# Sums of squares over the partitions: one product in single precision, or two products of the split type

## The chip, the cores and the metric

One core of a Trainium2 chip runs the whole program. The metric is the device time of one execution in microseconds (us); several executions are timed and their median is quoted. One further execution is recorded by the hardware profiler, with its instructions, its waits and its transfers. All durations below come from that one record.

## The reference, cut to what matters

The program is one layer of an encoder on 2,176 tokens (2,048 of a prompt, 128 of running streams) of width 1,024. Every row norm has the same form:

```python
def rmsnorm(x, g):
    xf = x.astype(jnp.float32)
    y = xf * lax.rsqrt(jnp.mean(xf * xf, axis=-1, keepdims=True) + RMS_EPS)
    return (y * g.astype(jnp.float32)).astype(x.dtype)
```

A token is normed before the input projection; the attention output and the pooling mixer's output are normed separately before they go into one output projection; the sum with the residual is normed before a squared-ReLU network of width 4,096; its result is normed before a gate; and the final result is normed once more. Everything is float32.

## The kernel before, in words

Tokens lie along the free axis and channels over the 128 partitions, so a sum of squares over channels is a sum over partitions and over tiles. All weights and activations of the large products are split into a high part (rounded to the type fp32r) and a low part (the rest), and `mm3` (L166 to L171) makes each product as three fp32r products: high by high, low by high, high by low. `split` (L179 to L181) makes the two parts: ScalarE (ACT) copies into the high part (L180), and VectorE (DVE) or GpSimd (POOL) subtracts (L181).

The program has two stages. **Stage A** goes over six blocks of tokens (one of 256, five of 384): `load_norm` (L251) loads and norms, then the input projection, attention, the pooling mixer, and `out_proj` (L275). A string (L27) lays out by hand in which order the pieces of the blocks are written. In its last letters the mixer of block 5 (`B5`) and the attention's rest of block 5 (`A5`) come ahead of the last piece of the output projection of block 4 (`O4`). **Stage B** works on six parts (four of 368 tokens, two of 352), in three pairs: an up projection that combines blocks of weights and activations (`up`), a down projection, a tail with the gate, and a finish that norms and writes out. The tail of one pair lies beside the up projection of the next.

The class `SumSq` does every norm's sum. `add` (L188): ACT squares a tile into a temporary `sqt` (L198), POOL or DVE adds it to the accumulator `sqa` (L199). When all tiles are in, `rstd` (L226) or `rstd_dve` (L201) adds over the partitions: TensorE (PE) multiplies by a matrix of ones (L229, L204) into a bank of PSUM called `ms`, of which there is one. Then comes the reciprocal root: in `rstd_ps`, ACT takes a logarithm (L236) and an exponential (L237) and DVE corrects in three steps (L238 to L240); in `rstd_dve`, DVE does it all in eleven steps (L208 to L215).

There are 35 such sums: five in the prologues of blocks 1 to 5, three in each of six output projections (`out_ra`, `out_rb` and the sum of the projected rows, two of the last kind run in stage B), six of the tail's and six of the finish, of which three go by `rstd_dve` and three by `rstd`. Block 0's prologue makes its products in a line of its own (L659).

Temporaries rotate through a fixed number of buffers by tag, in the order in which the program is written: `sqt` has 2 (the up projection's `v` takes from the same two), `sqa` 5, the rows of x (tag `xr`) 4, and `rt` 2 (the root's temporaries, shared with operands of `up`). A tile can be written only when the earlier tile of its buffer has been read for the last time. The order of each engine's instructions is not the program's: a scheduler lays it out from its own model of durations, within the dependencies and the rotation. Once laid out, an engine runs its list strictly in order. All loads stand in one list, that of SyncE (SP).

## Time and profile before

| | us |
|---|---|
| median of 3 runs (2475.68 to 2479.82) | 2478.29 |
| the profiled execution | 2475.05 |
| its span, first to last instruction | 2473.3 |
| PE busy in the span | 2341.9 (95%) |
| DVE busy | 1718.6 (69%) |
| POOL busy | 1154.7 (47%) |
| ACT busy | 1027.8 (42%) |

The span is what the profile can explain; 1.75 us lie outside it. PE is busy nearly everywhere, so a stretch is read by where PE is not: stage A (to about 780 us), the step from stage A to stage B (690 to 780), the two changeovers between pairs (about 1325 to 1400 and 1905 to 1965), and the end (from 2452).

### The profile page before, as it was taken

What the parts mean: (1) busy time and instruction counts of PE and PEld (TensorE: products, weight loads), DVE (VectorE), ACT (ScalarE), POOL (GpSimd) and SP (SyncE); (2) the same over time, 40 slices, a digit from 0 to 9 for tenths busy, and PEclk for the clock granted to TensorE, in tenths of its full rate; (3) what the DMA queues carried; (4) which work ended last, traced back from release to release, by engine and by line L of the source; (5) the groups of instructions that cost most, each with busy time, mean ns of one, the idle gap of its engine ahead of it and who ended that gap; (6) DMA issues with size and microseconds to landing.
All of it is one profiled execution on the core that took longest, in us unless ns stands there. A gap on an engine that the chain in (4) does not pass through costs nothing. (4 is left out here: it accounts for less than half of the span.)

```text
span 2473.3 us, 39045 instructions
## 1 busy us (share of the span) xinstructions
PE 2341.9 (95%) x13748; PEld 2258.1 (91%) x13748; DVE 1718.6 (69%) x3050; ACT 1027.8 (42%) x2139; POOL 1154.7 (47%) x964
## 2 busy tenths in 40 slices
PE   7879898999979999999998999999999899999996
PEld 7868797788879999999998999999999899999996
DVE  6866678767858777766677777776577866666565
ACT  5545555445633333332454333333365223333364
POOL 5734355434565444433475344443277333333275
PEclk9989999999999999999999999999999999999998
DMA  7554586688482334432455234342355522222233
GB/s 181 166 190 154 160 271 204 219 284 298 151 300 94 112 122 125 126 94 69 163 188 166 93 124 123 121 133 73 128 184 148 159 69 76 74 73 69 86 99 107
DMA packets 235443, 356.99 MB, mean 144 GB/s; under 512 B 43120, under 2 KB 119664, under 8 KB 235248
## 3 DMA queue, kind: packets, MB, share of 16 engines
q1 hardware_dynamic: 234704, 353.78, 45.5%
q8 instruction: 109, 1.79, 0.3%
q14 instruction: 86, 0.70, 0.1%
q10 hardware_dynamic: 544, 0.72, 0.1%
HBM read 284.86 MB, written 69.55 MB: 143 GB/s over the span
## 5 line engine op out<-in xcount | busy, mean ns | idle before, releaser
L181 POOL TENSOR_TENSOR wlo<-wraw,whi 128x512 fp32r<-128x512 f32 x277 | 380.9, 1381 | 308.6 <-ACT whi L180 234.0
L169 PE MATMUL ps_dn<-hh,whi 128*128 128x368 f32 (+1 forms) x1536 | 505.6, 329 | 8.4 <-DVE acc L881 7.6
L170 PE MATMUL ps_dn<-hh,wlo 128*128 128x368 f32 (+1 forms) x1536 | 503.6, 328 | 0.0
L171 PE MATMUL ps_dn<-hl,whi 128*128 128x368 f32 (+1 forms) x1536 | 501.3, 327 | 0.0
L180 ACT CAST whi<-wraw 128x512 fp32r<-128x512 f32 x436 | 267.7, 618 | 308.7 <-PE ps_dn L171 89.3
L881 DVE TENSOR_TENSOR acc<-ps_dn,acc 128x368 f32<-128x368 f32 (+1 forms) x384 | 201.5, 530 | 268.1 <-PE ps_dn L171 266.6
L181 POOL TENSOR_TENSOR wlo<-A,whi 128x512 fp32r<-128x512 f32 x96 | 126.9, 1322 | 383.8 <-ACT whi L180 278.6
L169 PEld LDWEIGHTS ps_dn<-hh,whi 128*128 128x128 f32 x1536 | 288.3, 188 | 17.4 <-DVE acc L881 16.3
L170 PEld LDWEIGHTS ps_dn<-hh,wlo 128*128 128x128 f32 x1536 | 288.4, 188 | 0.6 <-DVE wlo L181 0.3
L171 PEld LDWEIGHTS ps_dn<-hl,whi 128*128 128x128 f32 x1536 | 288.4, 188 | 0.3
L180 ACT CAST whi<-A 128x512 fp32r<-128x512 f32 x192 | 118.7, 620 | 271.3 <-PE ps_dn L171 185.8
L169 PE MATMUL ps_in<-xnh,whi 128*128 128x384 f32 (+1 forms) x480 | 164.8, 343 | 19.7 <-DVE z L698 10.3
L199 POOL TENSOR_TENSOR sqa<-sqa,sqt 128x384 f32<-128x384 f32 (+3 forms) x119 | 132.4, 1114 | 91.5 <-ACT sqt L198 83.0
L180 ACT CAST whi<-S 128x512 fp32r<-128x512 f32 x144 | 89.2, 619 | 183.7 <-PE ps_dn L171 133.2
L170 PE MATMUL ps_in<-xnh,wlo 128*128 128x384 f32 (+1 forms) x480 | 162.0, 337 | 0.3 <-DVE wlo L181 0.3
L171 PE MATMUL ps_in<-xnl,whi 128*128 128x384 f32 (+1 forms) x480 | 161.1, 337 | 0.3 <-DVE xnl L246 0.3
L181 DVE TENSOR_TENSOR wlo<-wraw,whi 128x512 fp32r<-128x512 f32 x159 | 139.1, 875 | 17.4 <-ACT whi L180 15.4
L817 POOL TENSOR_TENSOR S<-A,S 128x512 f32<-128x512 f32 x48 | 62.8, 1308 | 139.8 <-DVE wlo L181 139.8
L170 PE MATMUL ps_gt<-x2h,wlo 128*128 128x368 f32 (+1 forms) x384 | 126.6, 330 | 0.0
L169 PE MATMUL ps_gt<-x2h,whi 128*128 128x368 f32 (+1 forms) x384 | 126.1, 328 | 0.0
L171 PE MATMUL ps_gt<-x2l,whi 128*128 128x368 f32 (+1 forms) x384 | 125.5, 327 | 0.0
L181 DVE TENSOR_TENSOR wlo<-S,whi 128x512 fp32r<-128x512 f32 x144 | 105.7, 734 | 21.0 <-ACT whi L180 17.1
(254 smaller groups left out, 6341.6 us busy)
## 6 DMA issues: line engine op xcount, KB each, us to landing
A<-in_w_up SPq DMA_DIRECT2D x192, 256.0 KB, 2.7
wraw<-in_w_down SPq DMA_DIRECT2D x192, 256.0 KB, 2.6
wraw<-in_w_gate SPq DMA_DIRECT2D x96, 256.0 KB, 2.7
wraw<-in_w_out SPq DMA_DIRECT2D x64, 256.0 KB, 3.4
wraw<-in_w_in SPq DMA_DIRECT2D x60, 256.0 KB, 3.9
x<-in_xT SPq DMA_DIRECT2D x40, 192.0 KB, 3.8
xr<-in_xT SPq DMA_DIRECT2D x40, 192.0 KB, 3.6
x1d<-xr SPq DMA_DIRECT2D x40, 192.0 KB, 3.1
```

What stands on the lines that cost most here:

```text
L169: nc.tensor.matmul(ps, lhsT=whl.hi(wk), rhs=xh, start=first and i == 0, stop=False)
L170: nc.tensor.matmul(ps, lhsT=whl.lo(wk), rhs=xh, start=False, stop=False)
L171: last_mm[0] = nc.tensor.matmul(ps, lhsT=whl.hi(wk), rhs=xl, start=False, stop=last and i == n - 1).ins
L180: nc.scalar.copy(out=hi, in_=src)
L181: lo_eng.tensor_tensor(out=lo, in0=src, in1=hi.bitcast(F32), op=ALU.subtract)
L199: eng.tensor_tensor(out=o, in0=o, in1=t, op=ALU.add)
L817: nc.gpsimd.tensor_tensor(out=raw[o], in0=raw[a], in1=raw[b], op=op)
L881: nc.vector.tensor_tensor(out=a, in0=ps, in1=a, op=ALU.add)
```

## The change

Both products with the ones matrix go through a new method `total`. It takes two tiles of tag `sqt`, splits the accumulator into them, with the subtraction on DVE, and multiplies each by a ones matrix of type fp32r, accumulating in the same bank. The ones are now made by a memset into a `sqt` tile and a cast; block 0's own products go on with the same bytes read as float32. `total` has no other caller than these two.

```diff
-    ones = const.tile([P, P], F32, name="ones")
+    ones_r = const.tile([P, P], F32R, name="ones_r")
+    ones = ones_r.bitcast(F32)
+    one_f = tmp.tile([P, NMAX], F32, tag="sqt", name="one_f", bufs=2)[:, :P]
     eps_t = const.tile([P, 1], F32, name="eps_t")
-    nc.vector.memset(ones, 1.0)
+    nc.vector.memset(one_f, 1.0)
+    nc.vector.tensor_copy(out=ones_r, in_=one_f)
...
+        def total(self, ps):
+            h, l = (
+                tmp.tile([P, NMAX], F32R, tag="sqt", name="sq" + c, bufs=2)[:, : self.n] for c in "hl"
+            )
+            split(self.acc[:, : self.n], h, l, nc.vector)
+            nc.tensor.matmul(ps, lhsT=ones_r, rhs=h, start=True, stop=False)
+            nc.tensor.matmul(ps, lhsT=ones_r, rhs=l, start=False, stop=True)
+
         def rstd_dve(self, dim, pstile):
...
-            nc.tensor.matmul(ps, lhsT=ones, rhs=self.acc[:, :n], start=True, stop=True)
+            self.total(ps)
...
         def rstd(self, dim, pstile):
...
-            nc.tensor.matmul(ps, lhsT=ones, rhs=self.acc[:, :n], start=True, stop=True)
+            self.total(ps)
```

By count, PE has 70 fp32r products in place of 35 in single precision, ACT 35 casts more (`sqh`), DVE 35 subtractions (`sql`) and one cast more; POOL and SP issue as many as before. Lines behind the method stand 11 further down in the new kernel (L293 is the old L282), those between the constants and the method 3. The laid-out orders differ in many places, since the scheduler works from other durations and other rotations. Three of them matter here.

**SP at the step from stage A to stage B.** The operand tiles of the first up projection (`B21h` to `T4l`, 0.75 MB each) and the rows of x for the output projection (`xr`, 0.2 MB each). Before:

```order
L803 DMA B21h<-cd0B21h 128x1472
L803 DMA B21l<-cd0B21l 128x1472
L803 DMA T1h<-cd0T1h 128x1472
L803 DMA T1l<-cd0T1l 128x1472
L134 DMA wraw<-in_w_out 128x512
L803 DMA T3h<-cd0T3h 128x1472
L803 DMA T3l<-cd0T3l 128x1472
L134 DMA wraw<-in_w_out 128x512
L803 DMA B22h<-cd0B22h 128x1472
L803 DMA B22l<-cd0B22l 128x1472
L803 DMA T4h<-cd0T4h 128x1472
L803 DMA T4l<-cd0T4l 128x1472
L282 DMA xr<-in_xT 128x384
```
After:

```order
L814 DMA B21h<-cd0B21h 128x1472
L814 DMA B21l<-cd0B21l 128x1472
L814 DMA T1h<-cd0T1h 128x1472
L814 DMA T1l<-cd0T1l 128x1472
L293 DMA xr<-in_xT 128x384
L814 DMA T3h<-cd0T3h 128x1472
L293 DMA xr<-in_xT 128x384
L814 DMA T3l<-cd0T3l 128x1472
L293 DMA xr<-in_xT 128x384
L814 DMA B22h<-cd0B22h 128x1472
L293 DMA xr<-in_xT 128x384
L814 DMA B22l<-cd0B22l 128x1472
L814 DMA T4h<-cd0T4h 128x1472
L814 DMA T4l<-cd0T4l 128x1472
```
Four rows of x now stand between the operand tiles, all behind the first four tiles, where one stood behind all ten. The loads of `acc` that stood ahead of the operand tiles stand behind them.

**ACT at the same place**, with the tiles' numbers. Before, around the mixer's sum of block 5 (`sqa_7175`, L236), whose squares of the output projection (`sqt`) stand partly ahead:

```order
L437 ACTIVATE sqb_7242<-ps_b_7238,cv_sb_73 128x384
L440 ACTIVATE mxh_7172<-ps_b_7238,pgain_139 128x384
L198 ACTIVATE sqt_8026<-xr_7991 128x384
L180 CAST whi_8152<-wraw_8150 128x512
L180 CAST whi_8196<-wraw_8194 128x512
L236 ACTIVATE sqa_7175<-ps_ms_7248,eps_t_76 128x384
L237 ACTIVATE rs_t_7250<-sqa_7175 128x384
```
After, the same sum (`sqa_7272`), from the mixer's last activation on:

```order
L448 ACTIVATE sqb_7339<-ps_b_7335,cv_sb_73 128x384
L451 ACTIVATE mxh_7269<-ps_b_7335,pgain_141 128x384
L183 CAST sqh_7346<-sqa_7272 128x384
L201 ACTIVATE sqt_7828<-xr_7793 128x384
L247 ACTIVATE sqa_7272<-ps_ms_7345,eps_t_77 128x384
L201 ACTIVATE sqt_7878<-xr_7843 128x384
L248 ACTIVATE rs_t_7352<-sqa_7272 128x384
L201 ACTIVATE sqt_7928<-xr_7893 128x384
L201 ACTIVATE sqt_7978<-xr_7943 128x384
L201 ACTIVATE sqt_8028<-xr_7993 128x384
```
The split's cast `sqh_7346` now stands ahead of six squares of the output projection of block 4, whose buffers come behind it in the rotation.

**DVE at the end of the program**, from the tail's last part on (`L955`, now `L966`). Before:

```order
L955 TENSOR_TENSOR sg<-ps_gt,sqa 128x352
L208 TENSOR_SCALAR sqa<-ps_ms 128x352
L957 TENSOR_TENSOR sg<-ps_ple,sg 128x352
L209 TENSOR_SCALAR rs_t<-sqa 128x352
L959 TENSOR_TENSOR acc<-acc,sg 128x352
L213 SCALAR_TENSOR_TENSOR rs_t<-sqa,rs_t 128x352
L214 TENSOR_TENSOR rs_t<-rs_t 128x352
L199 TENSOR_TENSOR sqa<-sqa,sqt 128x352
L215 SCALAR_TENSOR_TENSOR rs_t<-rs_t 128x352
```
After:

```order
L966 TENSOR_TENSOR sg<-ps_gt,sqa 128x352
L968 TENSOR_TENSOR sg<-ps_ple,sg 128x352
L970 TENSOR_TENSOR acc<-acc,sg 128x352
L202 TENSOR_TENSOR sqa<-sqa,sqt 128x352
L184 TENSOR_TENSOR sql<-sqa,sqh 128x352
L219 TENSOR_SCALAR sqa<-ps_ms 128x352
L184 TENSOR_TENSOR sql<-sqa,sqh 128x352
L220 TENSOR_SCALAR rs_t<-sqa 128x352
L224 SCALAR_TENSOR_TENSOR rs_t<-sqa,rs_t 128x352
L225 TENSOR_TENSOR rs_t<-rs_t 128x352
```
The first step of the even part's root (L208, now L219) stood ahead of the tail's last additions; it now stands behind the last of them (L202) and a subtraction `sql`, and the rest of the chain behind a second `sql`. The same holds at the two changeovers: there, too, L219 stands behind the last square's addition and the `sql`, and from L220 on the chain runs in one piece.

## Rows read from the trace of the kernel before

**Rows 1.** The page's head: the span, and PE's busy time with its share and instructions.

```profile
span 2473.3 us, 39045 instructions
...
PE 2341.9 (95%) x13748; PEld 2258.1 (91%) x13748; DVE 1718.6 (69%) x3050; ACT 1027.8 (42%) x2139; POOL 1154.7 (47%) x964
```

**Rows 2.** Stretches: their us, busy time by engine, PE's clock, DMA share, GB/s.

```profile
250.00:690.00 440.00, 404.55 (x2227) 360.06 (x2227) 320.25 (x736) 234.31 (x602) 209.43 (x211) 0.97 0.70 226
690.00:780.00 90.00, 75.27 (x398) 71.07 (x399) 64.36 (x87) 32.23 (x60) 54.57 (x43) 0.94 0.61 219
780.00:1325.00 545.00, 541.15 (x3208) 536.24 (x3208) 373.58 (x580) 205.87 (x380) 255.41 (x193) 1.00 0.40 125
```

**Rows 3.** All records of the ones products on PE: ns shortest/median/longest.

```profile
L229 PE MATMUL ps_ms<-sqa,ones x64: 377/486/1009, 53.0 to 2457.1; 128*128 128x384 f32 x40, 128*128 128x368 f32 x12, 128*128 128x256 f32 x6, 128*128 128x352 f32 x6
L204 PE MATMUL ps_ms<-sqa,ones x6: 459/471/472, 1331.0 to 2452.6; 128*128 128x368 f32 x4, 128*128 128x352 f32 x2
```

**Rows 4.** Timeline of PE around one ones product: start, us, instruction.

```profile
1331.03 0.78 PE L204 MATMUL ps_ms<-sqa,ones 128*128 128x368 f32 x2
...
1331.82 0.33 PE L170 MATMUL ps_up<-B11h,wlo 128*128 128x368 f32 x1
...
1331.98 0.33 PE L171 MATMUL ps_up<-B11l,whi 128*128 128x368 f32 x1
```

**Rows 5.** Waits of PE in the bank's products: engine awaited, total, times, longest.

```profile
PE ps_ms L229 <- DVE sqa L238: 7.6, 4, 3.5
```

**Rows 6.** Groups by form in stage A: a split's two parts, busy and mean ns.

```profile
L181 DVE TENSOR_TENSOR mxl<-dt,mxh 128x384 fp32r<-128x384 f32 x20 | 14.2, 710 | 2.9 <-ACT mxh L180 2.9
...
L180 ACT CAST mxh<-dt 128x384 fp32r<-128x384 f32 x20 | 10.2, 509 | 19.6 <-DVE dt L427 19.6
```

**Rows 7.** DVE's additions of the squares: ns shortest/median/longest.

```profile
L199 DVE TENSOR_TENSOR sqa<-sqa,sqt x42: 517/911/1620, 1253.8 to 2455.8; 128x368 f32<-128x368 f32 x28, 128x352 f32<-128x352 f32 x14
```

**Rows 8.** Timelines of SP, POOL and PE at the step between the stages.

```profile
686.34 0.97 SPq L889 DMA_DIRECT2D acc<-x1d  x2
...
696.75 0.39 SPq L803 DMA_DIRECT2D B21h<-cd0B21h  x1
...
710.03 0.33 SPq L282 DMA_DIRECT2D xr<-in_xT  x1
...
722.15 0.99 POOL L292 TENSOR_TENSOR xr<-xr,ot 128x384 f32<-128x384 f32 x1 [8.90 <-issue]
...
724.35 0.66 PE L169 MATMUL ps_ob<-mxh,whi 128*128 128x384 f32 x1 [7.32 <-ACT sqt L198]
```

**Rows 9.** Short stretches at that step, columns as in rows 2.

```profile
706.00:716.00 10.00, 10.00 (x60) 10.00 (x59) 4.96 (x8) 3.54 (x6) 5.50 (x5) 1.00 1.02 412
716.00:724.00 8.00, 1.03 (x6) 0.71 (x5) 0.82 (x2) 0.23 (x1) 0.99 (x1) 0.85 1.03 388
```

**Rows 10.** Timelines of DVE, ACT and PE at the first changeover.

```profile
1332.99 0.53 DVE L208 TENSOR_SCALAR sqa<-ps_ms 128x368 f32<-128x368 f32 x1
...
1345.99 0.53 DVE L215 SCALAR_TENSOR_TENSOR sqa<-rs_t 128x368 f32<-128x368 f32 x1
...
1346.56 0.47 ACT L847 COPY x<-ps_up 128x368 f32<-128x368 f32 x1 [4.42 <-DVE sqa L215]
...
1347.08 0.67 PE L169 MATMUL ps_up<-T3h,whi 128*128 128x368 f32 x1 [5.54 <-ACT x L847]
```

**Rows 11.** Timelines of DVE and PE at the end of the program.

```profile
2453.14 0.52 DVE L208 TENSOR_SCALAR sqa<-ps_ms 128x352 f32<-128x352 f32 x1
...
2455.76 0.52 DVE L199 TENSOR_TENSOR sqa<-sqa,sqt 128x352 f32<-128x352 f32 x1
...
2456.33 1.54 PE L229 MATMUL ps_ms<-sqa,ones 128*128 128x352 f32 x2 [3.22 <-DVE sqa L199]
...
2458.98 0.53 DVE L214 TENSOR_TENSOR rs_t<-rs_t 128x352 f32<-128x352 f32 x1
2459.54 0.52 DVE L215 SCALAR_TENSOR_TENSOR sqa<-rs_t 128x352 f32<-128x352 f32 x1
```

## Prediction, made before the changed kernel had run

> **What bounds the kernel now.** The head of the page comes first: PE is busy for 2341.9 of 2473.3 us [rows 1], so a product saved on PE is worth something only where PE runs without a gap, and anything else counts only where PE stands still. The stretches say where that is. From 780 to 1325 us PE is busy for 541.15 of 545 us at full clock; the stretch of the second pair has the same form. In stage A it is busy for 404.55 of 440 us, about 92%, and around the step between the stages for 75.27 of 90 [rows 2]. Then come the waits of PE, where the sums themselves show: four products of the `ms` bank waited 7.6 us together for the last reading of the bank by the sum before [rows 5]. Last the timelines of the four places where PE stands for long: the step between the stages (a stop of 7.32 us) [rows 8], the two changeovers (5.54 us at the first) [rows 10], and the end, where there is nothing to do but the chain of the root [rows 11]. The change touches all of them, because what it adds (a cast, a subtraction, two square buffers) stands in front of each root.
>
> **What a product costs and what a split costs.** A sum in single precision is recorded as two passes: 64 and 6 records, so 35 products [rows 3]. The pair of 1331.03 and one fp32r product fill the time to 1331.82, that is 0.79 us; an fp32r product takes 541.15 / 3208 = 0.169 us on average in the full stretch [rows 2, 4]. So the old product takes 0.79 - 0.17 = 0.62 us and two new ones 0.33: 0.29 us saved for each sum, 35 x 0.29 = 10.2 us at most. The split that stands in front costs a cast of 0.51 us and a subtraction of 0.71 us, which are means of the same forms in stage A [rows 6]. The subtraction reads two tiles of SBUF; the additions of squares on DVE, of the same form, take 0.52 to 1.62 us with a median of 0.91 [rows 7], so 0.5 and 1.6 are its bounds. From the accumulator's last addition to the first step of the root the new way is therefore some 0.5 + 0.7 - 0.3 = 0.9 us longer. On PE that is nothing as long as other products stand between.
>
> A rule speaks against the change here. The additions of rows 7 have a shortest time of 0.52 us and a longest of 1.62, three times as much. The Trainium skill, page "SBUF — State Buffer", section "Who interferes with whom", says that a DVE instruction with both inputs in SBUF and a GpSimd instruction that reads SBUF share a port pair as an exclusive lock, so that the later one blocks entirely; the spread of rows 7 agrees. By that rule alone each new subtraction beside POOL would take about 1.6 us, and a changeover would cost 0.9 us more than I put below (1.8 us for both); I stay with 0.71 us, since the forms of rows 6 ran in the same company.
>
> **Sums under a full PE.** Eight sums (two of the output projection's, six of the tail's) have products all round them in stage B. There the split lies beside PE's work, and the saving counts whole: 8 x 0.29 = -2.3 us. If the cover went, one sum would cost its 0.9 us instead.
>
> **Sums of stage A.** Twenty sums of the prologues, the mixer, the attention and the first output projections: 20 x 0.29 = -5.8 us if PE were always full. It is at 92%, and the same engines carry the split: DVE 320.25 and ACT 234.31 of 440 us [rows 2]. Two new things work against it. The products now stand in the list behind a cast and a subtraction, and the square buffers of the split make later squares wait. The nearest row is the wait for the bank, 1.9 us each time it occurs [rows 5]: some ten more of those less half the saving would be about +10 us. I take -4 us, and -5.8 to +10 as ends.
>
> **The step between the stages.** Before, the sum of the mixer of block 5 had six squares of the output projection ahead of it or free of it. Now its cast stands ahead of them in ACT's list, since the two square buffers rotate in the order of the program. The rows of x that these squares free (four buffers) come free later, so the loads of later rows move behind the first four operand tiles. The trace of before shows what that is worth. There one row of x was issued at 710.03, behind ten tiles of 0.75 MB that began at 696.75; POOL could use it at 722.15, and PE stood for the 7.32 us up to 724.35 [rows 8]. Meanwhile the transfers ran at 412 and 388 GB/s [rows 9], so this stop is a stop for transfers. With the new list, and T the issue of the first operand tile: the first row stands behind 3.0 MB, at 0.38 MB per us it lands at T + 8.4 (3.2 MB); PE, which can run two projected rows past a missing one, has 7 of 16 rows done and stops for it. Four rows (24 products of 0.174 us at 384 columns, so 4.2 us a row) reach T + 25.2. The next row stands behind all ten tiles, four rows of x, four large and some small loads, 12.6 MB, and lands at T + 33.2: a second stop of 8 us. Five more rows take 21 us, to T + 54.2. Before, from the first of the later loads at 686.34, the same work ended with three rows after 724.35, near 737, which is 50.7 us later. When T falls is not in the trace: the tiles of stage A whose buffers they take are free between 682 and 690. With T = 687 the new end is 741.2, +4.3 us. After the stop PE ran at half speed (0.66 us beside 0.33 [rows 8]) for some 12 products; a second stop adds 12 x 0.17 = 2.1 us. So +6.4 us. The ends: if T = 682 and the second row comes early, both stops vanish and the old one (7.4 us and 2.1 us of slow products) with them, -9.5; if T = 690 and the transfers run at 0.345 MB/us, as the 12.3 MB between 686.34 and 722.15 did, it is +12 and a second row of stops makes +20.
>
> **The changeovers.** In the first, the chain of the even part's root runs from 1332.99 to 1345.99 + 0.53, with the tail's own work in between; the last step frees the buffer for `x`, ACT copies at 1346.56, PE goes on at 1347.08 [rows 10]. Now the first step stands behind the tail's last addition, the `sql` and the products, so it starts near 1340 and not at 1333, but then nothing else lies in its way: eleven steps, which follow one another at 0.56 us (2458.98 to 2459.54 [rows 11]), and a subtraction or two of the up projection's weights, 11 x 0.56 + 0.4 to 1.7 = 6.6 to 7.9 us, to 1346.6 to 1347.9. That is +0.7 us, and twice, +1.4. PE's gain on the two products there is swallowed by the same stop. The odd part's products now fall into the up projection, where PE has no gap: 2 x 0.33 = +0.7 us.
>
> **The end.** Before, the even part's root began at 2453.14 and ended at 2459.54 + 0.52, with the odd part's last addition (2455.76) and product (2456.33) inside it [rows 11]. Now it begins behind that addition: 2455.7 + 0.5, a subtraction of 0.55 us, two products at half clock and their end, so the first step is at 2457.4; a second subtraction; the second step at 2458.45; nine steps of 0.56 us: 2463.85. That is 2463.85 - 2460.06 = +3.8 us, and nothing hides it, since the writing out hangs on it. Bounds +3.1 and +4.5.
>
> **Sum.** -2.3 - 4 + 6.4 + 1.4 + 0.7 + 3.8 = +6.0 us on the profiled execution of 2475.05 us, so 2481. The median of the runs is 3.2 us higher; on it, 2478.3 + 6.0 = 2484.
>
> **The rivals.** (a) The step between the stages costs nothing: the second row comes in time, as it does if the large loads behind the tiles are issued later than the x rows are freed. Then the sum is -0.4 us, 2478. For it: the old stop of 7.4 us goes and one of about that size comes. Against it: the transfers are at their limit there [rows 9]. (b) The faster side: both stops vanish, since four rows of x now stand between the tiles and not behind all of them; -9.5 in place of +6.4 is a sum of -9.9, 2468. It decides from T below 683. (c) The plain reading: each sum's 0.29 us counts everywhere and every split is covered, -10.2 us, 2468. Against it stand the end and the changeovers, where the chain lies bare. (d) More of the same on the slow side: the square buffers also hold back the squares of other blocks in stage A, so that its sums cost +10 and not -4: +20, 2498. For it: bank and squares already make PE wait [rows 5]. Against it: ACT is busy only half of stage A [rows 2].
>
> **How the numbers follow.** About 5 us (0.2%) is what a measurement of this kernel can tell from no change, so "same" is 2473.3 to 2483.3. The forecast has 0.48, most of it above that bound (0.44, and 0.04 within it); (a) 0.21, within; (b) 0.10 and (c) 0.08, faster; (d) 0.13, slower. Together: faster 0.18, same 0.25, slower 0.57. The range from 2468 to 2500 reaches to the centres of (b), (c) and (d) and leaves half of each out. The forecast's own range is 2478 to 2492.
>
> **What would show it.** Right: in the changed profile two stops of PE for `xr` or its squares between 690 and 745, and the first `ps_up` of the pair later by 4 to 9 us; the first root step of the end behind the last addition of squares, near 4 us from its old distance to the end; changeover stops of 5.5 to 7 us; the stretch 780 to 1325 shorter by about 1 us. Wrong: one stop or none at the step, or stage A's stops for the bank grown or gone by more than 6 us; or the last root's chain starting, as before, ahead of the last addition.

## The result and the profile after

The changed kernel takes 2498.34 us (median; 2494.30 to 2502.92), the kernel before in the same company 2479.06 us (2475.68 to 2481.21). The recorded ratio of the two is 1.0089, with a 95% interval of 1.0070 to 1.0108: 17 to 27 us slower. (The two medians quoted differ by 19.3 us, the two profiled executions by 22.9.) The forecast was slower by 6 us. The sign was right and the time lies inside the wide range, but the size is off by a factor of three to four.

The profiled execution of the changed kernel took 2497.97 us, its span is 2496.2. Its page, beside [rows 1]:

```profile
span 2496.2 us, 39144 instructions
...
PE 2342.1 (94%) x13748; PEld 2267.8 (91%) x13748; DVE 1741.4 (70%) x3086; ACT 1037.5 (42%) x2174; POOL 1151.7 (46%) x964
```

PE's busy time is the same to 0.2 us, although 35 products are cheaper by 0.29 us each; in sum the 22.9 us are time in which PE stood. In stage A, where 20 of the 35 sums are, PE was busy for 608 us at a granted clock of 0.93, and before for 607 at 0.95, so the cheaper products don't show there. A table of stretches at fixed times doesn't show where, since the two programs drift apart. So I line them up by work: at which time each had issued the same number of product columns, the sums' own products left out. The lead of one over the other changes only where something happens:

| stretch (time in the kernel before) | forecast | measured, changed minus before |
|---|---|---|
| stage A, 0 to 682 | -4 | +0.8 |
| step between the stages, 682 to 817 | +6.4 | +9.9 |
| full stretches of stage B (817 to 1317, 1467 to 1909, 2031 to 2452) | -2.3 | +3.4 (+1.4, +1.3, +0.7) |
| first changeover, 1317 to 1467 | +0.7, and +0.3 of the odd part | +4.5 |
| second changeover, 1909 to 2031 | +0.7, and +0.3 | +0.6 |
| end, from the last gate product | +3.8 | +3.7 |
| sum | +6.0 | +22.9 |

The waits of PE say what it stood for (engine awaited, total, times, longest), first in the changed kernel, then a row of the kernel before:

```profile
PE ps_ob L172 <- DVE ot L302: 20.0, 3, 11.6
PE ps_up L172 <- ACT x L858: 17.6, 3, 8.2
...
PE ps_ms L209 <- ACT sqh L183: 10.9, 4, 3.9
...
PE ps_ms L210 <- DVE sql L184: 5.0, 7, 1.4
PE ps_ms L209 <- DVE sqa L249: 4.8, 1, 4.8
```

```profile
PE ps_ms L229 <- DVE sqa L199: 5.1, 3, 3.2
```

The two `ps_ms` rows on `sqh` and `sql`, 15.9 us in 11 waits, are new: PE now waits for the split itself. They take the place of the old row on `sqa` L199, three waits for the last addition of squares, 5.1 us. The old row for the bank's last reader [rows 5] has 4.8 us in place of 7.6. Of the first row 11.57 us are the step between the stages and 7.37 a stop in stage A (at 519.37); of the second 16.45 are the two changeovers.

The step between the stages, timelines of SP, ACT and PE (start, us, engine, instruction, and in brackets the idle time before it and what ended it), beside [rows 8]:

```profile
686.42 0.33 SPq L814 DMA_DIRECT2D B21h<-cd0B21h  x1
...
688.70 0.52 SPq L293 DMA_DIRECT2D xr<-in_xT  x1
...
686.43 0.51 ACT L183 CAST sqh<-sqa 128x384 fp32r<-128x384 f32 x1 [1.39 <-POOL sqa L450]
...
699.36 0.52 ACT L201 ACTIVATE sqt<-xr 128x384 f32<-128x384 f32 x1 [8.36 <-DVE xr L306]
...
687.00 0.69 PE L209 MATMUL ps_ms<-sqh,ones_r 128*128 128x384 f32 x1 [3.39 <-ACT sqh L183]
...
699.85 0.69 PE L172 MATMUL ps_ob<-mxh,whi 128*128 128x384 f32 x1 [11.57 <-DVE ot L302]
...
716.31 0.52 PE L172 MATMUL ps_oa<-mxh,whi 128*128 128x384 f32 x1 [4.05 <-DVE ot L305]
...
727.08 0.66 PE L172 MATMUL ps_ob<-mxh,whi 128*128 128x384 f32 x1 [2.70 <-ACT sqt L201]
```

PE stood for 3.39 us until the cast, for 11.57 until a row of x that was issued at 688.70 behind four operand tiles, and then for 4.05 and 2.70: 21.7 us in place of one stop of 7.32 and one of 1.90.

The first changeover, timelines of DVE and PE, beside [rows 10]:

```profile
1350.18 0.53 DVE L202 TENSOR_TENSOR sqa<-sqa,sqt 128x368 f32<-128x368 f32 x1
1350.82 1.45 DVE L184 TENSOR_TENSOR sql<-sqa,sqh 128x368 fp32r<-128x368 f32 x1
1352.18 1.75 DVE L184 TENSOR_TENSOR wlo<-A,whi 128x512 fp32r<-128x512 f32 x1
1353.86 0.53 DVE L219 TENSOR_SCALAR sqa<-ps_ms 128x368 f32<-128x368 f32 x1
...
1359.89 0.54 DVE L226 SCALAR_TENSOR_TENSOR sqa<-rs_t 128x368 f32<-128x368 f32 x1
...
1360.99 0.67 PE L172 MATMUL ps_up<-T3h,whi 128*128 128x368 f32 x1 [8.23 <-ACT x L858]
```

The end of the program, timeline of DVE, beside [rows 11]:

```profile
2474.64 0.52 DVE L202 TENSOR_TENSOR sqa<-sqa,sqt 128x352 f32<-128x352 f32 x1 [0.73 <-ACT sqt L201]
2475.27 0.53 DVE L184 TENSOR_TENSOR sql<-sqa,sqh 128x352 fp32r<-128x352 f32 x1
2476.55 0.53 DVE L219 TENSOR_SCALAR sqa<-ps_ms 128x352 f32<-128x352 f32 x1 [0.75 <-PE ps_ms L210]
...
2482.26 0.53 DVE L226 SCALAR_TENSOR_TENSOR sqa<-rs_t 128x352 f32<-128x352 f32 x1
```

Each chain begins behind the last addition of squares (L202) and a `sql`, as the forecast had it.

### The profile page after: what moved, and what is told of

The parts are those of the page before. It is cut to its first block, busy times and chain, and to the rows that moved or that the text cites. A ratio compares the mean times of both kernels' runs of the same rounds, so it can differ in the third digit from the quotient of the medians.

```text
span 2496.2 us, 39144 instructions
## 1 busy us (share of the span) xinstructions
PE 2342.1 (94%) x13748; PEld 2267.8 (91%) x13748; DVE 1741.4 (70%) x3086; ACT 1037.5 (42%) x2174; POOL 1151.7 (46%) x964
## 4 chain that ended last, share of the span: by engine, by line
PE 41%; DVE 11%; issue 2%; ACT 2%; DMA 1%; POOL 0%; SPq 0%; POOLq 0%; ACTq 0%; DVEq 0%
PE ps_dn L172 6%; PE ps_dn L173 6%; PE ps_dn L174 6%; PE ps_up L172 6%; PE ps_up L174 6%; PE ps_up L173 6%; DVE wlo L184 2%; DVE x2l L257 1%; PE ps_gt L174 1%; PE ps_gt L173 1%; PE ps_gt L172 1%; DVE acc L892 1%; DVE acc L970 1%; DVE cl L184 1%; ACT x2h L256 1%
## 5 line engine op out<-in xcount | busy, mean ns | idle before, releaser
L172 PEld LDWEIGHTS ps_dn<-hh,whi 128*128 128x128 f32 x1536 | 288.7, 188 | 21.7 <-DVE acc L892 19.7
L202 POOL TENSOR_TENSOR sqa<-sqa,sqt 128x384 f32<-128x384 f32 (+3 forms) x119 | 128.6, 1081 | 98.3 <-ACT sqt L201 90.2
```

The source lines that it names most:

```text
L172: nc.tensor.matmul(ps, lhsT=whl.hi(wk), rhs=xh, start=first and i == 0, stop=False)
L202: eng.tensor_tensor(out=o, in0=o, in1=t, op=ALU.add)
```

## The experiments

Two theories run through all of them. Theory R: the split's two tiles take both square buffers, and this tie moves the split behind squares, or squares behind the split, in the laid-out order. Theory S: the cast and the subtraction cost their time in front of the product, wherever their tiles lie. Where one stretch is quoted, it is the profiled execution's lead at equal work, as in the table above; totals are medians, each with the kernel before on the same chip.

One caution on single executions. Five kernels below (e7, e8, e9, e10, e13) have, but for the constants, the lists of the kernel before on all engines up to 680 us. There, at equal work, their profiled executions stood between 3.6 us ahead of it and 11.2 us behind it (e8). Of these 11.2 us 10.1 are busy time of PE, at a lower granted clock (the end of stage A before, then in e8: us, busy times, and in the third column from the end the clock):

```profile
0.00:681.96 681.96, 607.18 (x3418) 544.24 (x3419) 490.83 (x1131) 360.76 (x915) 328.47 (x340) 0.95 0.66 207
```

```profile
0.00:693.20 693.20, 617.29 (x3418) 553.36 (x3419) 491.39 (x1132) 358.97 (x914) 327.38 (x340) 0.93 0.65 204
```

So a single execution says nothing about a few us in stage A. Later stretches repeat better, though not to 1 us. Five other executions with the lists of the kernel before from 830 to 1930 us (e2, e4, e5, e9, e14) were 0 to 1.9 us longer than it in the first full stretch, 0.4 to 3.1 us in the three together, and -0.5 to +2.8 us in the first changeover. So the table's +3.4 for the full stretches is not told apart from no change, and what it shows is that no gain came; of its +4.5 for the first changeover up to 2.8 can be chance.

### One sum: the mixer's of block 5

The same change with that one sum in other buffers:

```diff
+        own5[0] = lambda c: pa.tile([P, HIST + NMAX], F32R, tag="pt", name="sq" + c, bufs=2)
...
     def out_rb(b):
-        state[b]["rb"] = state[b]["sqb"].rstd(512, ps_tile(TAGS[3], "ps_ms"))
+        state[b]["rb"] = state[b]["sqb"].rstd(512, ps_tile(TAGS[3], "ps_ms"), own5[0] if b == 5 else None)
```

> The changed kernel, but the two split tiles of one sum, the mixer's of block 5, come from the two buffers of the mixer's own temporaries and not from the two square buffers. Its cast, subtraction and two products stay. Theory R (the square buffers tie the split to the squares of the output projection, so the rows of x and their loads come late): the list of loads is laid out as in the kernel before, the step between the stages costs +0 to +2 us against the kernel before, not +8 to +11, and the total is near 2489 us. Theory S (the split itself, a cast and a subtraction in front of the product, makes PE stop there): the step stays at +8 to +11 and the total near 2498.

Measured: 2484.69 us beside 2474.89, ratio 1.0043 (1.0028 to 1.0058), against 1.0089 for the changed kernel. The step between the stages costs +4.5 us (-0.4 at 682, +4.1 at 817) and not +9.9. That lies between what the two theories gave (0 to 2, and 8 to 11); the other sums at this place are still split in the square buffers. The largest stop there is the old one:

```profile
725.96 0.66 PE L172 MATMUL ps_ob<-mxh,whi 128*128 128x384 f32 x1 [6.35 <-ACT sqt L201]
```

Then that sum alone, on the kernel before, first in the square buffers (an argument `new` chooses for each sum between `total` and the old product):

```diff
     def out_rb(b):
-        state[b]["rb"] = state[b]["sqb"].rstd(512, ps_tile(TAGS[3], "ps_ms"))
+        state[b]["rb"] = state[b]["sqb"].rstd(512, ps_tile(TAGS[3], "ps_ms"), new=b == 5)
```

> The kernel before, with one sum changed: the mixer's of block 5 is split and uses the square buffers. Theory R: this one sum brings the late loads and the stops at the step between the stages, +8 to +11 us there, total 2487 to 2490. Theory S, or no tie at all: one split costs 0.9 us at most, total 2478 to 2480.

Measured: 2487.29 us, ratio 1.0053 (1.0035 to 1.0072), 13 us slower. One of 35 sums costs over half of the whole loss. From 680 us to 817 it falls behind from +2.0 to +14.9. The largest part is the stop for rows of x, 9.6 us longer than before; shorter stops ahead of it, up to 3.07 us, make the rest:

```profile
730.93 0.66 PE L172 MATMUL ps_ob<-mxh,whi 128*128 128x384 f32 x1 [16.96 <-ACT sqt L201]
```

And the same sum alone, with the two tiles in the mixer's temporaries:

```diff
-        state[b]["rb"] = state[b]["sqb"].rstd(512, ps_tile(TAGS[3], "ps_ms"))
+        state[b]["rb"] = state[b]["sqb"].rstd(512, ps_tile(TAGS[3], "ps_ms"), own=pt_r[0] if b == 5 else None, new=b == 5)
```

> The kernel before with one sum split, the mixer's of block 5, as in the second run, but with its two tiles in the buffers of the mixer's temporaries and not in the square buffers. Theory R (the tie to the squares): the list of loads is as before, the step between the stages costs -2 to +2 us, the total is within 3 us of the kernel before; the second run was 13 us above it. Theory S (the split in front of the product): 8 us and more above.

Measured: 2473.69 us beside 2476.12, ratio 0.9991 (0.9970 to 1.0012). The same cast, subtraction and products, with nothing but two other buffers, cost nothing in sum (-0.2 us from 682 to 817). Theory R holds for this step, and theory S is out as the cause of the 13 us. The sum does hide a price of the split: PE waits for the cast and for the low part (timeline of PE),

```profile
692.14 0.44 PE L212 MATMUL ps_ms<-sqh,ones_r 128*128 128x384 f32 x1 [1.12 <-ACT sqh L183]
693.99 0.69 PE L213 MATMUL ps_ms<-sql,ones_r 128*128 128x384 f32 x1 [1.41 <-DVE sql L184]
```

and the old stop of 7.32 us is not there (the longest is now 2.82), since the list of loads isn't quite the one before: a row of x, issued at 701.91, stands ahead of the last two operand tiles.

### The finish: changeovers and end

Low parts in a buffer of their own in stage B (there is room for one):

```diff
-            h, l = (
-                tmp.tile([P, NMAX], F32R, tag="sqt", name="sq" + c, bufs=2)[:, : self.n] for c in "hl"
-            )
+            h = tmp.tile([P, NMAX], F32R, tag="sqt", name="sqh", bufs=2)[:, : self.n]
+            l = (own[0] or sqt_r)("sql")[:, : self.n]
...
+        own[0] = lambda nm: pb.tile([P, NMAX], F32R, tag="sqs", name=nm, bufs=1)
```

> The changed kernel, but in stage B the low part of every split has a buffer of its own (there is room for one), so that it no longer waits for the last square of the tail. Theory R: at the end the first root step of the even part goes back ahead of the last addition of squares, and the end costs 0 to +1.5 us against the kernel before and not +3.8; the two changeovers together +1 to +2 and not +4.9; total 2491 to 2493, the step between the stages unchanged. Theory S: the two subtractions and casts stand in the chain anyway, the end stays at +3 to +4 and the total within 2 us of 2498.

A miss: 2505.18 us beside 2474.89, ratio 1.0123 (1.0102 to 1.0143), worse than the changed kernel, with the end as late as there (24.3 us from the last gate product; the kernel before has 21.1, the changed one 24.8). The order of ACT shows why it can't decide: the high part still takes a square buffer, and its cast still stands behind the last square. The run separates nothing at the end, and the single buffer ties consecutive splits to one another. It loses the 8 us in stage B: of its profiled execution's +34.8 us the full stretches have 10.2 and the second changeover 4.6. Why was not followed further.

The kernel of e1 again, with the six finish sums put back to the old product:

```diff
-                rs = sqs[h].rstd_dve(D, ps_tile("ms", "ps_ms"))
+                rs = sqs[h].rstd_dve(D, ps_tile("ms", "ps_ms"), new=False)
```

(and `rstd_load` likewise).

> The run with the mixer's sum of block 5 in buffers of its own, and besides the six sums of the finish as in the kernel before (one product in single precision, no split). Theory: the split in front of the finish's bare chains costs 3.8 us at the end and 1.5 to 3 us at the two changeovers, so this run is 5 to 7 us under that one, 3 to 6 us above the kernel before. Rival (the changeovers and the end are late for another reason, such as the stops before them): less than 3 us under it.

Measured: 2478.78 us beside 2477.27, ratio 1.0005 (0.9991 to 1.0019); with the split finish it was 1.0043. That is 9 us less, more than expected. The end is back to 21.1 us; the rest lies within what the totals resolve. The finish sums alone, on the kernel before:

```diff
-            rs = state[b]["sq1"].rstd(D, ps_tile("ms", "ps_ms"))
+            rs = state[b]["sq1"].rstd(D, ps_tile("ms", "ps_ms"), new=False)
```

(and likewise for all but the finish).

> The kernel before with only the six sums of the finish split. Theory: +3.8 us at the end, +0.7 to +2.5 us at each changeover, nothing elsewhere: 5 to 8 us above the kernel before. Rival (the first changeover's 4.5 us of the changed kernel come from the split alone): 9 us and more above.

Measured: 2479.84 us beside 2477.27, ratio 1.0016 (0.9997 to 1.0034), 4 us where 5 to 8 were expected. The end has 24.6 us, +3.5; the changeovers are +1.1 and -0.2. So the first changeover's +4.5 of the changed kernel is not the split's price: with the same split it was +0.7 in e1 and +1.1 here. In e2, whose finish is the old one, it was +2.8.

Now the same sums, untied on both tiles: they take the four buffers of the embedding's parts (`row_p`), which are free by then.

```diff
-                rs = sqs[h].rstd_dve(D, ps_tile("ms", "ps_ms"))
+                rs = sqs[h].rstd_dve(D, ps_tile("ms", "ps_ms"), own=lambda c: row_p("sq" + c, n))
```

All 35 sums split, the six of the finish and the mixer's of block 5 untied:

> All 35 sums split as in the changed kernel, but seven of them without the square buffers: the mixer's of block 5 in the mixer's temporaries (as in the first run) and the six of the finish in the four buffers of the embedding's parts. At the end the first root step of the even part stands ahead of the last addition of squares again. Theory R (the tie to the squares makes the end late): from the last gate product to the end of the span 0 to +1.0 us against the kernel before, where the changed kernel has +3.8; the first run's total minus 3 to 5 us, 5 to 8 us above the kernel before. Theory S (the cast and the subtraction in the bare chain): the end stays at +3 to +4, the total as in the first run, 10 to 11 us above.

Measured: 2478.10 us beside 2474.43, ratio 1.0017 (1.0003 to 1.0031). The end is 21.15 us from the last gate product, as before the change. The root's chain stands among the tail's work again, both `sql` included (timeline of DVE at the end):

```profile
2459.95 0.51 DVE L222 TENSOR_SCALAR sqa<-ps_ms 128x352 f32<-128x352 f32 x1
...
2463.06 0.52 DVE L202 TENSOR_TENSOR sqa<-sqa,sqt 128x352 f32<-128x352 f32 x1
...
2464.49 0.52 DVE L184 TENSOR_TENSOR sql<-sqa,sqh 128x352 fp32r<-128x352 f32 x1
...
2466.59 0.53 DVE L229 SCALAR_TENSOR_TENSOR sqa<-rs_t 128x352 f32<-128x352 f32 x1
```

The two changeovers are 1.9 us *shorter* each than in the kernel before (PE's timeline at the first; the stop for `x` is 2.97 us where [rows 10] has 5.54):

```profile
1351.35 0.66 PE L213 MATMUL ps_ms<-sql,ones_r 128*128 128x368 f32 x1 [1.59 <-DVE sql L184]
...
1354.98 0.67 PE L172 MATMUL ps_up<-T3h,whi 128*128 128x368 f32 x1 [2.97 <-ACT x L864]
```

And the six finish sums alone, untied, on the kernel before:

> The kernel before with only the six sums of the finish split, and their two tiles in the four buffers of the embedding's parts, not in the square buffers. Theory R: each changeover about 2 us shorter than in the kernel before, the end as before (21.1 us from the last gate product), so 3 to 4 us under the kernel before; the run with the same sums in the square buffers was 4 us above. Rival (the changeovers of the twelfth run were shorter for another reason, such as what stood before them): changeovers within 0.7 us of before, the total within 2 us.

Measured: 2472.48 us beside 2475.89, ratio 0.9982 (0.9965 to 1.0000). With e9 (0.9991) it is one of two versions whose time is under both kernels', by 4 us with an interval that touches zero. Its profile shows the changeovers 1.4 and 0.4 us shorter and the end as before; the second changeover loses part of it to a stop of 1.86 us for `acc` later on. So the tie alone made the end late; the split in itself costs nothing there.

### The sums under a full PE

Only the eight sums split that have products round them in stage B:

```diff
     def out_fin(b):
-        rs = state[b]["sq1"].rstd(D, ps_tile("ms", "ps_ms"))
+        rs = state[b]["sq1"].rstd(D, ps_tile("ms", "ps_ms"), new=b >= 4)
```

(the tail's six with `total`, all others with the old product).

> The kernel before with only the eight sums split that lie under a full PE in stage B: six of the tail's norm and two of the projected rows. The forecast's term: 8 x 0.29 = 2.3 us under the kernel before. Rival (in the changed kernel PE waited 0.5 to 1.4 us for the low part in seven of these products, because the scheduler places both products together before the subtraction has ended): 1 to 3 us above the kernel before.

Measured: 2482.63 us beside 2477.27, ratio 1.0024 (1.0009 to 1.0039): slower, where the forecast has a gain of 2.3 us. PE waits for the low part in four of the eight sums: 1.44 us at 790, and 0.52, 0.53 and 1.00 us in the second sums of the three pairs. The expectation put this down to the list, which would hold both products next to each other. That is not so: in these three, four, four and three other products stand between the two. But the subtraction took 1.60 to 1.64 us, beside a weight's subtraction on POOL, where 0.71 was forecast and 0.54 would have been in time (DVE and PE, the second sum of the first pair):

```profile
1260.05 1.63 DVE L184 TENSOR_TENSOR sql<-sqa,sqh 128x368 fp32r<-128x368 f32 x1
...
1261.74 0.44 PE L213 MATMUL ps_ms<-sql,ones_r 128*128 128x368 f32 x1 [0.52 <-DVE sql L184]
```

At 790 the subtraction took 0.54 us; there it stands too late in DVE's list.

The same with the low part left out:

```diff
-            nc.tensor.matmul(ps, lhsT=ones_r, rhs=h, start=True, stop=False)
-            nc.tensor.matmul(ps, lhsT=ones_r, rhs=l, start=False, stop=True)
+            nc.tensor.matmul(ps, lhsT=ones_r, rhs=h, start=True, stop=True)
```

> The eight sums under a full PE, as in the run with them alone, but the low part is left out: a cast and one product each, no subtraction, so the sums of squares are only as exact as the type's high part. Theory (PE loses time there by waiting for the low part): the waits in these products go, stage B's full stretches are 1 to 4 us shorter than in the kernel before (8 x 0.45 = 3.6 us of product less), and 3 to 6 us shorter than in the run with both parts. Rival (the loss comes from DVE being late elsewhere, by its list's new order): the stretches stay as in the run with both parts.

Measured: 2478.73 us beside 2476.12, ratio 1.0012 (0.9993 to 1.0032). The waits for `sql` are gone, and the three full stretches are nearly as long as with both parts: 529.7, 444.3 and 417.6 us where both parts have 530.1, 443.6 and 418.4 and the kernel before 527.2, 442.4 and 417.8. In place of the wait for `sql` PE now stands for weights that POOL splits, five times in these stretches, 2.8 us together, which is what six products less save there (6 x 0.45 = 2.7). Two of the five:

```profile
1258.06 0.44 PE L173 MATMUL ps_gt<-x2h,wlo 128*128 128x368 f32 x1 [0.51 <-POOL wlo L184]
...
1260.87 0.44 PE L173 MATMUL ps_ple<-pth,wlo 128*128 128x368 f32 x1 [0.54 <-POOL wlo L184]
```

This was the rival's outcome (the stretches stay), though the rival gave DVE's list as the reason: here POOL's splitting of the weights is nearly as late as PE, and what PE saves it waits for at the next weights.

Then a product without anything in front. The last addition writes its result as fp32r (the low part is left out), in the 17 sums of the prologues, the tail's norm and the finish:

```diff
+                if fin:
+                    r = tmp.tile([P, NMAX], F32R, tag="sqt", name="sqr", bufs=2)[:, :n]
...
-                eng.tensor_tensor(out=o, in0=o, in1=t, op=ALU.add)
+                eng.tensor_tensor(out=r, in0=o, in1=t, op=ALU.add)
```

> The low part is left out here too, and the cast with it: the last addition of squares writes its result as the product's type, so no instruction is added, and one product of 0.17 us takes the place of 0.62 us, in the 17 sums of the prologues, the tail's norm and the finish; the other 18 are as before. Theory (what stands in front of the product decides, not its price): nothing stands in front now, so the end costs -0.3 to -1.0 us, the changeovers 0 to -1, the full stretches -2 to -3, the total is 3 to 7 us under the kernel before. Rival (the buffer tie or the new order gives that back too): within 2 us of the kernel before.

Measured: 2480.60 us beside 2476.12, ratio 1.0014 (0.9995 to 1.0032). From 790 us to the end it is 2.3 us shorter than the kernel before (changeovers -1.3 each, end -0.2, the full stretches +0.5 together), so where the chains lie bare it does about what was expected; the full stretches again have no gain. The total is not under the kernel before (3 to 7 us were expected): the time up to 790 us takes more than that back.

### Stage A

Only sums of stage A, without block 5's mixer and attention:

```diff
-        state[b]["ra"] = state[b]["sqa"].rstd(512, ps_tile(TAGS[3], "ps_ms"))
+        state[b]["ra"] = state[b]["sqa"].rstd(512, ps_tile(TAGS[3], "ps_ms"), new=b < 5)
```

(`out_rb` likewise, `out_fin` with `b < 4`, stage B old).

> Of the 35 sums only those of stage A are changed, without the mixer's and the attention's of block 5: five prologues, ten of mixer and attention, four of the projected rows, 19 in all. If the saving of 0.29 us for each product comes through as forecast, stage A ends 3 to 5.5 us earlier and the total is 2474 to 2476. If the order of stage A gives it back (the changed kernel was up to 9 us ahead there at 50 to 370 us and level at 680), the total is 2478 to 2481.

Measured: 2478.32 us beside 2474.89, ratio 1.0016 (0.9999 to 1.0033). A gain of 4 us is outside the interval. The changed kernel and this one share four stops that the kernel before doesn't have, here in this run (timeline of PE):

```profile
271.60 0.58 PE L212 MATMUL ps_ms<-sqh,ones_r 128*128 128x256 f32 x1 [4.80 <-DVE sqa L252]
...
374.33 0.45 PE L212 MATMUL ps_ms<-sqh,ones_r 128*128 128x384 f32 x1 [3.34 <-ACT sqh L183]
...
520.32 0.69 PE L172 MATMUL ps_ob<-mxh,whi 128*128 128x384 f32 x1 [7.26 <-DVE ot L305]
...
637.26 1.54 PE L585 MATMUL ps_tr<-ident,pm 128*128 128x128 f32 x6 [5.91 <-DVE pm L570]
```

The kernel before has others instead, 6.61 us at 383.74 (for `mxh`) and 3.52 at 637.26 (for the bank). Of the four the first waits for the bank, the second for the cast, the last for the softmax. The third waits for `ot`, the reader of the mixer's bank, and that stands late in the list of DVE (timeline of DVE in this run):

```profile
513.85 0.54 DVE L184 TENSOR_TENSOR cl<-xc,ch 128x368 fp32r<-128x368 f32 x1 [3.45 <-DMA cd0B22l<-cl]
...
514.91 0.41 DVE L545 CUSTOM_DVE_ANT_0 pm<-ps_sc,mask 128x256 f32<-128x256 f32 x1
...
518.18 1.15 DVE L184 TENSOR_TENSOR mxl<-dt,mxh 128x384 fp32r<-128x384 f32 x1
...
519.72 0.54 DVE L305 TENSOR_TENSOR ot<-ps_ob,sqa 128x384 f32<-128x384 f32 x1
```

Ahead of it stand a `cl` that waits 3.45 us for the store of an operand tile, eight softmax pieces of 0.41 us and a `mxl`. In the kernel before the reader of this place stands ahead of the softmax pieces (timeline of DVE):

```profile
521.40 0.55 DVE L291 TENSOR_TENSOR ot<-ps_ob,sqa 128x384 f32<-128x384 f32 x1
521.87 0.41 DVE L531 CUSTOM_DVE_ANT_0 pm<-ps_sc,mask 128x256 f32<-128x256 f32 x1
```

The same with the mixer's and attention's sums untied (the `own=pt_r[0]` of e9 for every block, and the mixer's of block 5 split too):

> As the run with stage A alone (19 sums split, stage B's sums and the attention's of block 5 as before, and now the mixer's of block 5 split too), but the split tiles of all mixer and attention sums come from the two buffers of the mixer's temporaries, not from the two square buffers. Theory R (the tie to the squares gives stage A's saving back): stage A ends 3 to 6 us before the kernel before, the total is 2 to 5 us under it. Rival (the split's cast and subtraction, or the lower clock after other stops, give it back wherever the tiles lie): the total is 0 to 5 us above the kernel before, as in the run with stage A alone.

Measured: 2487.08 us beside 2477.27, ratio 1.0040 (1.0021 to 1.0059): worse. The stop for the cast is gone, but the third is 11.39 us, again at `ot` behind softmax pieces (from 522.81 on, `ot` at 533.10). So theory R does not hold for these sums. The nine others, of the prologues and the projected rows, keep the square buffers here; untying them was not tried. Last, these nine alone, still in the square buffers:

> The kernel before with only nine sums of stage A split: five prologues and the projected rows of blocks 0 to 3. Theory (the mixer's and attention's sums, whose split waits among the squares of the output projection, carry stage A's loss): no stop of 4 us and more at these sums, stage A 1 to 3 us shorter, total 1 to 3 us under the kernel before. Rival (any split in stage A re-lays the order at a loss): total 1 to 5 us above, as in the run with all of stage A.

Measured: 2480.48 us beside 2475.89, ratio 1.0012 (0.9997 to 1.0028). The four stops are not there; two others of 7.08 and 6.70 us are, at a transpose that waits for DVE's softmax and at the mixer's product. So every kernel that split sums in stage A had long stops in other places than the kernel before, and none was faster. The profiles show a gain that is lost again: at 520 us eight of the nine kernels with other sums in stage A (all but e5) were 5 to 14 us ahead of the kernel before at equal work, and at 680 between 3.9 us ahead and 8.3 behind. Executions with its own lists there were 2.0 ahead to 5.4 behind at 520.

## Why the prediction was right or wrong

**The size.** The sign and the main mechanism were right. Two terms that were put as gains, the sums under a full PE (-2.3) and those of stage A (-4), were none, and two costs, the step and the changeovers, were too small. Changed alone and by medians, the groups cost 13 us (mixer's sum of block 5, e2), 4 (finish, e7), 6 (under a full PE, e8) and 4 (19 sums of stage A, e4); such numbers need not add up, as each kernel has lists of its own. Of the signs named, the two groups of stops at the step and the late chain at the end came; the changeover stops were 8.2 us and not 5.5 to 7, and the full stretch was not shorter. By term:

**Product and split.** The product's price was right where PE runs without a gap: two new ones start 0.17 us apart (794.99 and 795.16). The subtraction was taken at 0.71 us; the 35 of the changed kernel took 0.42 to 1.64 with a median of 0.55:

```profile
L184 DVE TENSOR_TENSOR sql<-sqa,sqh x35: 416/550/1640, 50.0 to 2477.0; 128x384 fp32r<-128x384 f32 x20, 128x368 fp32r<-128x368 f32 x8, 128x352 fp32r<-128x352 f32 x4, 128x256 fp32r<-128x256 f32 x3
```

At the changeovers, where it counts, it took 1.45 and 1.43 us, and in the six sums of the tail 1.60 to 1.64. POOL was at work each time when it began (at the first changeover at a sum of weights, from 1350.34 for 1.52 us). The two at the end, where POOL was idle, took 0.53 and 0.52. The Trainium skill's rule from "SBUF — State Buffer", section "Who interferes with whom", with the longest of [rows 7], gave 1.6; I had weighed it and not followed it, and the trace agrees with it.

**Sums under a full PE (-2.3, measured +3.4).** The failed step is "the split lies beside PE's work, and the saving counts whole", and the term behind it that was mis-sized is the subtraction: 0.71 us taken, 1.60 to 1.64 measured in the tail's sums. PE's other products between the two cover less than that, so it waited 0.5 to 1.0 us (and 1.44 at 790, where DVE's list is late). And e10 shows that the saving would not have counted without that wait either. I had read "PE is busy all the time" as "PE alone sets the pace"; POOL's weights were within half a us of it.

**Stage A (-4, measured +0.8, and between 0 and +8 by e4's total).** It lies between the value taken and the end that I had named (+10). The step that failed is to price 20 sums one by one in a stage whose order a scheduler lays out anew. What is seen is how a new stop arises: DVE's list has the mixer's reader behind the softmax. What stays open is which dependency of the split moves it there. For the mixer's and attention's sums the tie was tested (e5) and is not it; for the prologues' and rows' sums it was not tested, and e14, with these alone in the square buffers, has long stops too.

**The step between the stages (+6.4, measured +9.9).** Cause and place were right, down to the issue of the first tile (686.42; forecast 687) and the two groups of stops. Two sizes were off. The first row of x was taken to land 8.4 us behind the first issue, and PE to go on with it. POOL had the row after 11.3 us (697.75) and PE went on after 13.4 (699.85): the work of POOL and DVE on the row in between, 2.1 us, which [rows 8] also has (722.15 to 724.35), was not in the sum. The other 2.9 us are the load's; in part the transfers began slower, with 297 GB/s up to 692 us and 412 behind it, where the sum has 380 throughout. What the rest is isn't shown. (Timeline of POOL; stretches with GB/s last.)

```profile
697.75 0.99 POOL L303 TENSOR_TENSOR xr<-xr,ot 128x384 f32<-128x384 f32 x1 [4.73 <-DMA xr<-in_xT]
```

```profile
686.00:692.00 6.00, 1.28 (x2) 0.58 (x2) 2.81 (x5) 3.37 (x7) 3.79 (x5) 0.50 0.84 297
692.00:700.00 8.00, 0.15 (x1) 0.15 (x1) 1.40 (x4) 0.52 (x1) 2.01 (x2) 0.50 1.01 412
```

And PE stood for 3.39 us for the cast itself, which the sum didn't have. The second stop was 6.75 us in two pieces (forecast 8). e2 and e9 show the cause: one sum, two buffers.

**Changeovers (+2.1, measured +5.1).** The chain started at 1353.86; at the lead of 12.1 us that is 1341.8 in the time of the kernel before (forecast: near 1340), since `sql` and the `wlo` behind it took 3.2 us and not 1.4. The stop grew by 2.7 us, not 0.7. At equal work that is little: in e1 and e7 the same stop of 8.2 us comes to +0.7 and +1.1 over the whole changeover, near the forecast. In the changed kernel 37 us later PE stood another 1.80 us for `acc`, where e1 has no such stop, and the lead grew by 3.0 us there. The same second stop is in e2 (1.91 us) and e14 (1.82), which have the lists and the finish of the kernel before at this place, so it isn't the split's. DVE is busy 8.9 to 10 us of 10 there, and what tips it is open.

**The end (+3.8, measured +3.7).** Right in size and step. What the forecast did not say is that it is the tie alone: with both tiles untied it is gone (e12, e13).

**The rivals.** (d), which gives the measured total, has the wrong mechanism: stage A did not cost +10. That the time lies in the range, which reaches so far because of (d), is luck. (a) and (b) are out, as PE stood for both groups of rows. (c), the plain reading, fails at every place where it was tried (e4, e8, e10).

## What to carry to other kernels

A temporary that takes its buffer from an existing ring adds a dependency on everything that rotates through that ring, and the laid-out order follows the ring, not the arithmetic: before pricing an edit, ask of each new tile who takes the next buffer. One sum of 35 cost 13 us that way, and with two other buffers nothing in sum. Price what is put in front of a product by its longest time on record, if another engine can slow it: here 1.6 us and not 0.7. A saving on the busiest engine counts only if the next engine behind it has slack at the same place; 95% busy doesn't say that.

## What the runs showed of the hardware that I had not expected

The same instruction lists gave stage A's end up to 15 us apart in six executions (3.6 us ahead of the kernel before to 11.2 behind it), and in the slowest of them 10.1 us were longer busy time of PE at a granted clock of 0.93 in place of 0.95. A stage whose clock differs from one execution to the next has to be judged by medians of many.

And a subtraction of two SBUF tiles on DVE took 0.52 to 0.53 us four times and 1.43 to 1.64 us eight times in stage B of the changed kernel (shapes 128x352 and 128x368, both times in both). The four had POOL idle; at the eight POOL was in the middle of an operation of its own when they began. In a bare chain such an operation should be priced at its long time. Where POOL began only after the subtraction had, it kept its short time: 0.55 us at 789.23 (128x384), which POOL joined 0.22 us later.
